# Context's Fourier part in seven steps, a transform and the gate's turns reordered, matrices by casting DMA

## The chip, the cores and the metric

The program runs on one core of a Trainium2 chip. The metric is device time in microseconds of one execution. The engines are TensorE (PE: matmuls, with weight loads as PEld), VectorE (DVE), ScalarE (ACT), GpSimd (POOL) and SyncE (SP). SP and POOL issue the DMAs here, each from a queue that goes in order. Line numbers such as L322 are those of the kernel before.

## The reference, cut to what matters

Two layers over 1024 latent tokens and 256 context tokens with 1024 channels. The first layer is projected once (`u @ w_in`); 512 channels go to a Fourier mix, three times 512 to a two-stage Hyena convolution. The second layer, neighbourhood attention, and the gated feed-forward parts lie behind what is changed.

```python
def fourier_mix(p):
    g = p.astype(jnp.float32).reshape(B_, L, FOURIER_GROUPS, FOURIER_GDIM).transpose(0, 2, 1, 3)
    f = jnp.fft.fft2(g, norm="ortho").real
    return f.transpose(0, 2, 1, 3).reshape(B_, L, FOURIER_CH).astype(p.dtype)

def hyena_mix(p, conv_w, conv_b, w1, b1, freq, w2, b2, w3, skip):
    z = short_conv(p, conv_w, conv_b).astype(jnp.float32)
    x1, x2, v = jnp.split(z, 3, axis=-1)
    filt = hyena_filters(L, w1, b1, freq, w2, b2, w3)
    v = x1 * long_conv(v, filt[:, 0], skip[0])
    v = x2 * long_conv(v, filt[:, 1], skip[1])
    return v.astype(p.dtype)

def mixer_ab(u, w_in, w_out, ...):
    p = u @ w_in
    y_f = fourier_mix(p[..., :FOURIER_CH])
    y_h = hyena_mix(p[..., FOURIER_CH:], ...)
    return jnp.concatenate([y_f, y_h], axis=-1) @ w_out
```

Both streams, latent and context, go through `mixer_ab` with the same weights. Context is the short one: 256 tokens.

## The kernel before, in words

Activations lie with channels on the 128 partitions and tokens along the rows. Matmul operands are split into a rounded high part (a copy on ScalarE, L326) and a rest (a subtraction on VectorE, L328), and each product is three matmuls: high by high, low by high, high by low.

The functions are Python generators. The order in which the builder draws from them is the order of the program, and so a priority; when the program is built, a scheduler fixes each engine's order and the buffers from it and from its own estimate of times. `follow(ins)` puts an instruction behind another one on the same engine, without a wait. On the chip every engine and queue takes its instructions strictly in the order fixed.

`in_proj` runs 16 blocks (steps 0 to 15) of 128 output channels. A step loads and splits a weight block, runs its 72 matmuls (`lin`), draws one step of the context filters (`filt`) and of the modulation vectors (`ada`), draws from `four` and `conv` from a given step on, and evicts its own result: blocks 0 to 3 for the Fourier part, the others through the short convolution (L814 to L818). Context's blocks 0 to 3 are stored to memory (`pd`).

`fourier_c` is context's Fourier part in four groups of 128 channels. For each group it loads two halves, folds them (`folded`), splits three operands, multiplies them by the channel matrix (`channels`), splits the three results, multiplies those by the position matrices, and evicts (`fourier_out`). All of a group is in one step; a last step multiplies the middle column (`middle`) and writes the results.

`conv` is context's long convolution: `forward_c` turns the operand (L899), then transforms two classes of frequencies, `cls` 0 and 1; `combine_c` multiplies by the filter's spectrum; `inverse_c` goes back. `o` is the first or second convolution. A class's matrices (`vf_c`) are loaded as float16 and cast on ScalarE: at L365 into S2 buffers for `o` 0, at L374 otherwise.

The latent long convolution begins with `turned` (L981), which transposes the operand into eight tiles and splits them. Eight `unit`s follow, each a class and a block of frequencies: a first half of the matmuls, a second half, then `combine_l` (L949 to L958), which loads the spectrum and multiplies, and `parts` (L970, L972), which splits. A unit of class 1 has 24 matmuls and two matrices, one of class 0 has 12 and one. After each unit of the first convolution a gate tile is turned (`turn_x`, L1006). `inverse_first` transforms back, applies the gate and forms the next operand; while it ends, the first four units of the second convolution are begun (first halves). `inverse_last` (L1111) ends the second convolution, with the latent Fourier part in it.

What matters of the buffers: S2 has 35 (512 words a row, whatever is asked for), S4 has 21 (1024 words), `wh` and `wl` two each, `ws` four (staging of float16 matrices and of weights); of the eight PSUM banks six are `ps` and two `pq`. Behind the projection `self.PS` gives `ps` alone, and `self.PQ` gives `pq`. `cmat` and `cmat2` load a float16 matrix into `ws` from SP and cast it on ScalarE (L374, L388) into `wh` or `wl`. `cast` has GpSimd issue a DMA that casts on its way into the buffer (L313).

Of the kernel before, what the change touches and what calls it, by code (L numbers as in the profile page):

```python
# [10 lines left out]
F32 = mybir.dt.float32  # L11
F32R = mybir.dt.float32r
# [6 lines left out]
P = 128  # L19
# [217 lines left out]
class Builder:  # L237
# [154 lines left out]
    def cast(self, w, src):  # L392

        self.mj = (self.mj + 1) % 4
        m = self.W(("wh", "ws", "wl", "ws")[self.mj], "mat", F32R, w)
        self.ldr(m, src)
        return m

# [422 lines left out]
    def in_proj(self, u, fill, four, conv):  # L821
# [14 lines left out]
        for i, nb in enumerate(order):  # L836
            wh, wl = self.weights(a["w_in"][nb])
            acc = self.lin(wh, wl, 0, range(KB), u, PCS)
            for g, n in fill:
                for _ in range(n[min(i, len(n) - 1)]):  # L840
                    next(g, None)
            if i > 5:
                next(four, None)
            if i > 13:
                next(conv, None)
# [45 lines left out]
    def forward_c(self, o):  # L891
        nc, a = self.nc, self.a
        ab = self.ab["c"]
        tr = []
        PS = self.PS if o == 0 else self.PQ
        for j in (0, 1):
            ps = PS()
            for cb in range(4):
                nc.tensor.transpose(ps[:, cb * P:(cb + 1) * P], ab[cb][:, j * P:(j + 1) * P], self.ident)  # L899
            hi, lo = self.twin(o)  # L900
            self.split(ps, hi, lo)
            tr.append((hi, lo))
        yield
        for cls in (0, 1):
            spec = []
            for i in (cls, 2 + cls):
                xh, xl = tr[(i + i // 2) % 2]
                mt = self.cmat(256, a["vf_c"][i, 0], small=o == 0)
                ps = PS()
                self.mm(ps, mt[:, :P], xh, True, False)  # L910
                self.mm(ps, mt[:, :P], xl, False, False)
                self.mm(ps, mt[:, P:], xh, False, True)
                spec.append(ps)
            self.combine_c(o, cls, spec)
            yield
# [58 lines left out]
    def turned(self):  # L974

        nc = self.nc
        self.tr = []
        for j in range(8):
            ps = self.PS()
            for cb in range(4):  # L980
                nc.tensor.transpose(ps[:, cb * P:(cb + 1) * P], self.ab["l"][cb][:, j * P:(j + 1) * P], self.ident)  # L981
            hi, lo = self.S2(F32R), self.S2(F32R)
            self.split(ps, hi, lo)
            self.tr.append((hi, lo))
            yield
# [14 lines left out]
    def turn_x(self, k):  # L1000

        pc, rev, j = k // 4, k // 2 % 2, k % 2
        ps = self.PQ()
        for cb in range(4):
            x = (self.xrev if rev else self.xrow)[cb][:, j * P:j * P + P]
            self.nc.tensor.transpose(ps[:, cb * P:(cb + 1) * P], x, self.ident)  # L1006
        t = self.S2()
        self.nc.scalar.copy(t, ps)
        self.xt[(j, (0, 1, 2, 3)[2 * pc + rev])] = t

    def unit(self, o, fb, cls, bank=None):

        a = self.a
        tr = self.tr
        if cls == 0:
            src = a["vfe_l"][fb]
            mt = self.cast(1024, src) if o + fb == 0 else self.cmat(1024, src)
            mats = [mt[:, :512], mt[:, 512:]]
            q = 2 * (fb // 2)
            xs = [range(q, q + 2), range(4 + q, 6 + q)]  # L1020
        else:
            src = a["vfo_l"][fb]
            mats = [self.cast(1024, src[:, j * 1024:j * 1024 + 1024]) for j in (0, 1)] if o + fb == 0 else self.cmat2(src)
            xs = [range(4, 8), range(4)]
        bank = bank or self.PS
        spec = [bank(), bank()]
# [335 lines left out]
    def fourier_c(self, y):  # L1362
# [4 lines left out]
        for i in range(3):  # L1367
# [1 line left out]
            self.ldr(m[:, :256], a["fc_c"][i, 0])  # L1369
            self.ldr(m[:, 256:], a["fc_c"][i, 1])  # L1370
            mats[i] = m
        raws = []
        for g in range(4):
            p0, p1 = self.S2(F32, 128), self.S2(F32, 128)
            self.ld(p0, self.pd[g][:, 0:128])
            self.ld(p1, self.pd[g][:, 128:256])
            prs = self.folded(p0, p1, P, q[:, g:g + 1], qn[:, g:g + 1], nc.gpsimd)
            ae, ao, am = self.channels(prs, cg, 1, self.PS)
            ps = self.PS()
            for i, (xh, xl) in enumerate((ae, am, ao)):  # L1380
                m = mats[i]
                self.mm(ps[:, :256], xh, m[:, :256], i == 0, False)
                self.mm(ps[:, :256], xl, m[:, :256], False, False)
                self.mm(ps[:, :256], xh, m[:, 256:], False, i == 2)
            raw = self.S2()
            self.fourier_out(ps[:, 0:128], ps[:, 128:256], raw, P, self.T)
            raws.append(raw)
            yield
        self.middle(cgf, q, qn, mid, self.PS)
        for g in range(4):  # L1390
            nc.vector.tensor_copy(raws[g][:, P:P + 1], mid[:, g:g + 1])
            self.split(raws[g][:, :256], y.ap(0, g, 2), y.ap(1, g, 2))
# [771 lines left out]
    def run(self):  # L2164
# [119 lines left out]
                pass  # L2284

        self.banks = 6
        next(cc, None)
        self.xt, self.sums_due = {}, None
        for _ in self.turned():
            pass  # L2290
        for k, (fb, cls) in enumerate(((0, 1), (0, 0), (1, 1), (1, 0), (2, 1), (3, 1), (2, 0), (3, 0))):
# [2 lines left out]
            if k % 4 == 0:  # L2294
                self.gate_rows(k // 4)
            self.turn_x(k)
            if k == 6:
                next(cc)
        self.parts()
        units = [self.unit(1, fb, cls, self.PQ if k == 3 else None)  # L2300
                 for k, (fb, cls) in enumerate(((0, 1), (1, 1), (2, 1), (0, 0), (1, 0), (3, 1), (2, 0), (3, 0)))]
        for _ in range(2):
            next(cc)
# [259 lines left out]
```

## Time and profile before

| | |
|---|---|
| median of 3 runs | 2956.7 us (2954.18 to 2958.66) |
| the profiled execution's own time | 2957.89 us |
| its span, first to last instruction | 2956.0 us |
| mean granted TensorE clock | 0.984 |

In the views, times are microseconds from the span's start. A row of the timeline gives start, length, engine, line, operation, output and inputs by the program's names, shapes and count, and in brackets how long the engine had been idle and what released it. A row of the stages gives the busy time of PE, PEld, DVE, ACT and POOL, the granted clock, the share of the DMA engines and GB/s. The instructions that the change touches lie in about 290 to 640 us.

### The profile page before, as it was taken

The numbers are of one execution on the slowest core, as the hardware profiler recorded it, in microseconds if no ns is written. First come the engines' busy times: TensorE is split into PE (matmuls) and PEld (weight loads), VectorE is DVE, ScalarE is ACT, GpSimd is POOL, SyncE is SP. The second block draws the span as 40 slices with busy tenths as digits, with TensorE's granted clock in tenths as the row PEclk, the third lists the DMA queues.
The fourth block names the chain that finished last, engine by engine and source line by source line (L and its number), as shares of the span: only waits on it lengthen the run. The fifth ranks groups of instructions, "written<-read, shape, count | busy, mean of one in ns | idle before, by whom it ended". The sixth has DMA issues, their size and how long they took to land. (4 is left out here: it accounts for less than half of the span.)

```text
span 2956.0 us, 44485 instructions
## 1 busy us (share of the span) xinstructions
PE 2832.5 (96%) x15704; PEld 2363.7 (80%) x15704; DVE 2092.7 (71%) x3950; ACT 1330.1 (45%) x2490; POOL 529.2 (18%) x820
## 2 busy tenths in 40 slices
PE   8899898899999999999999999999999999999998
PEld 3678787788799888888888888788877688888886
DVE  6765666858777888966777437888777877764555
ACT  4543323543454333333455336677665533333433
POOL 2112012351100221222120002232212022111000
PEclk9999999999999999999999999999999999999999
DMA  9664433566556555659984345676756266434653
GB/s 336 219 210 161 144 102 127 185 222 225 199 176 199 193 202 202 219 189 323 309 305 153 129 130 154 174 183 168 221 169 226 75 240 227 168 111 167 227 194 128
DMA packets 303917, 568.41 MB, mean 192 GB/s; under 512 B 83144, under 2 KB 129930, under 8 KB 303694
## 3 DMA queue, kind: packets, MB, share of 16 engines
q1 hardware_dynamic: 242750, 373.11, 39.7%
q0 software_dynamic: 58640, 188.26, 17.8%
q10 hardware_dynamic: 2304, 4.20, 0.4%
q8 instruction: 124, 2.03, 0.3%
q14 instruction: 99, 0.81, 0.1%
HBM read 415.49 MB, written 119.80 MB: 181 GB/s over the span
## 5 line engine op out<-in xcount | busy, mean ns | idle before, releaser
L1605 PE MATMUL ps<-s,s 128*128 128x512 f32 x2008 | 498.3, 391 | 6.4 <-DVE s L1496 4.7
L1605 PEld LDWEIGHTS ps<-s,s 128*128 128x128 f32 x2008 | 377.6, 188 | 88.3 <-DVE s L1496 6.3
L322 PE MATMUL ps<-s,wh 128*128 128x256 f32 (+1 forms) x1584 | 358.7, 329 | 3.5 <-ACT wh L326 3.4
L322 PE MATMUL pq<-s,wh 128*128 128x512 f32 (+1 forms) x1040 | 316.2, 381 | 9.8 <-DVE s L1990 4.7
L322 PEld LDWEIGHTS ps<-s,wh 128*128 128x128 f32 x1584 | 265.8, 192 | 29.6 <-ACT wh L326 4.7
L322 PE MATMUL ps<-s,s 128*128 128x64 f16 (+3 forms) x2780 | 243.8, 241 | 31.1 <-DVE s L2099 8.8
L1777 PE MATMUL ps<-s,s 128*128 128x512 f32 (+1 forms) x1000 | 259.6, 383 | 3.1 <-DVE s L328 3.0
L328 DVE TENSOR_TENSOR wl<-ws,wh 128x1024 fp32r<-128x1024 f32 (+1 forms) x142 | 170.0, 1198 | 127.5 <-ACT wh L326 123.0
L326 ACT CAST wh<-ws 128x1024 fp32r<-128x1024 f32 (+1 forms) x142 | 145.8, 1027 | 241.2 <-PE ps L322 91.8
L326 ACT CAST s<-s 128x1024 fp32r<-128x1024 f32 (+2 forms) x184 | 168.1, 940 | 191.3 <-DMA s<-d 162.6
L322 PE MATMUL ps<-s,wl 128*128 128x256 f32 (+1 forms) x792 | 238.4, 327 | 2.7 <-DVE wl L328 2.7
L322 PEld LDWEIGHTS pq<-s,wh 128*128 128x128 f32 x1040 | 190.8, 191 | 47.5 <-DVE s L1990 5.9
L326 ACT CAST s<-t 128x512 fp32r<-128x512 f32 (+1 forms) x213 | 121.9, 587 | 220.9 <-PE ps L1605 81.2
L328 DVE TENSOR_TENSOR s<-s,s 128x1024 fp32r<-128x1024 f32 (+2 forms) x162 | 185.5, 1177 | 49.4 <-ACT s L326 46.9
L1777 PEld LDWEIGHTS ps<-s,s 128*128 128x128 f32 x1000 | 184.5, 188 | 41.2 <-DVE s L328 4.6
L322 PE MATMUL ps<-s,mat 128*128 128x512 f32 x714 | 180.3, 402 | 18.1 <-ACT s L326 10.9
L322 PE MATMUL pq<-s,wl 128*128 128x512 f32 (+1 forms) x520 | 196.3, 379 | 1.3 <-DVE wl L328 1.3
L328 DVE TENSOR_TENSOR s<-t,s 128x512 fp32r<-128x512 f32 (+1 forms) x213 | 136.9, 653 | 78.9 <-ACT s L326 51.0
L1605 PE MATMUL ps<-s,wh 128*128 128x512 f32 x608 | 189.1, 390 | 0.0
L322 PEld LDWEIGHTS ps<-s,mat 128*128 128x128 f32 x714 | 135.6, 193 | 54.9 <-ACT s L326 13.5
L322 PEld LDWEIGHTS ps<-s,s 128*128 128x128 f32 (+1 forms) x860 | 133.9, 196 | 45.3 <-ACT s L326 10.9
L322 PEld LDWEIGHTS ps<-s,wl 128*128 128x128 f32 x792 | 148.8, 191 | 16.4 <-DVE wl L328 3.6
(439 smaller groups left out, 5614.9 us busy)
## 6 DMA issues: line engine op xcount, KB each, us to landing
s<-d SPq DMA_DIRECT2D x283, 256.0 KB, 3.8
s<-in_down SPq DMA_DIRECT2D x150, 256.0 KB, 4.1
d<-s POOLq DMA_DIRECT2D x137, 256.0 KB, 3.3
s<-in_ada_w POOLq DMA_DIRECT2D x64, 512.0 KB, 5.2
d<-tk POOLq DMA_DIRECT2D x98, 256.0 KB, 3.6
g<-in_bias SPq DMA_DIRECT2D x128, 192.0 KB, 3.1
ws<-in_up SPq DMA_DIRECT2D x44, 512.0 KB, 3.9
d<-g POOLq DMA_DIRECT2D x87, 256.0 KB, 3.1
```

What stands on the lines that cost most here:

```text
L322: self.nc.tensor.matmul(o, l, r, start=st, stop=sp)
L326: self.last_hi = nc.scalar.copy(hi, src).ins
L328: self.last_lo = eng.tensor_tensor(lo, src, hi.bitcast(F32), SUB).ins
L1605: nc.tensor.matmul(ps, x[:, sl], y, start=first and j == 0 and x is wh and y is xh, stop=j == 3 and x is wl, skip_group_check=True)
L1777: m = nc.tensor.matmul(acc[j][:, c0:c1], x[:, sl], y[:, xs], start=first and k == 0, stop=last and k == 2, skip_group_check=True)
```

## The change

- Context's Fourier part begins one step earlier (step 5 instead of 6) and goes in seven steps: step k folds group k, multiplies group k-1 by the channel matrix and group k-2 by the position matrices, and evicts group k-3. The middle and the final splits are two further steps.
- `forward_c`'s class 1 of the first convolution is drawn after unit 1 instead of ahead of `turned`.
- The gate's turns are put behind the last transpose of `turned` on TensorE.
- `vf_c`'s matrices of the first convolution come by a casting DMA from GpSimd into S2. So do those of units 2 and 3 of the second convolution, into S4 (`cast4`), where SP and ScalarE brought them into `wh` and `wl`.
- Unit 7 of the second convolution, like unit 3, takes its banks from `pq`.

```diff
+    def cast4(self, src):
+
+        m = self.S4(F32R)
         self.ldr(m, src)
         return m
...
-            if i > 5:
+            if i > 4:
                 next(four, None)
             if i > 13:
                 next(conv, None)
...
-                mt = self.cmat(256, a["vf_c"][i, 0], small=o == 0)
+                if o == 0:
+                    mt = self.S2(F32R, 256)
+                    self.ldr(mt, a["vf_c"][i, 0])
+                else:
+                    mt = self.cmat(256, a["vf_c"][i, 0])
...
-                nc.tensor.transpose(ps[:, cb * P:(cb + 1) * P], self.ab["l"][cb][:, j * P:(j + 1) * P], self.ident)
+                last = nc.tensor.transpose(ps[:, cb * P:(cb + 1) * P], self.ab["l"][cb][:, j * P:(j + 1) * P], self.ident)
+            self.after_turned = last.ins
...
-            self.nc.tensor.transpose(ps[:, cb * P:(cb + 1) * P], x, self.ident)
+            with self.follow(self.after_turned):
+                self.nc.tensor.transpose(ps[:, cb * P:(cb + 1) * P], x, self.ident)
...
-    def unit(self, o, fb, cls, bank=None):
+    def unit(self, o, fb, cls, bank=None, wide=False):
...
-            mt = self.cast(1024, src) if o + fb == 0 else self.cmat(1024, src)
+            mt = self.cast4(src) if wide else self.cast(1024, src) if o + fb == 0 else self.cmat(1024, src)
...
-            mats = [self.cast(1024, src[:, j * 1024:j * 1024 + 1024]) for j in (0, 1)] if o + fb == 0 else self.cmat2(src)
+            half = [src[:, j * 1024:j * 1024 + 1024] for j in (0, 1)]
+            mats = [self.cast4(x) for x in half] if wide else [self.cast(1024, x) for x in half] if o + fb == 0 else self.cmat2(src)
...
-        raws = []
-        for g in range(4):
-            p0, p1 = self.S2(F32, 128), self.S2(F32, 128)
-            self.ld(p0, self.pd[g][:, 0:128])
-            self.ld(p1, self.pd[g][:, 128:256])
-            prs = self.folded(p0, p1, P, q[:, g:g + 1], qn[:, g:g + 1], nc.gpsimd)
-            ae, ao, am = self.channels(prs, cg, 1, self.PS)
-            ps = self.PS()
-            for i, (xh, xl) in enumerate((ae, am, ao)):
-                m = mats[i]
-                self.mm(ps[:, :256], xh, m[:, :256], i == 0, False)
-                self.mm(ps[:, :256], xl, m[:, :256], False, False)
-                self.mm(ps[:, :256], xh, m[:, 256:], False, i == 2)
-            raw = self.S2()
-            self.fourier_out(ps[:, 0:128], ps[:, 128:256], raw, P, self.T)
-            raws.append(raw)
+        raws, prs, opd, got = [], {}, {}, {}
+        for k in range(7):
+            if k >= 3:
+                raw = self.S2(F32, 256)
+                ps = got.pop(k - 3)
+                self.fourier_out(ps[:, 0:128], ps[:, 128:256], raw, P, self.T)
+                raws.append(raw)
+            if 0 <= k - 2 < 4:
+                ae, ao, am = opd.pop(k - 2)
+                ps = got[k - 2] = self.PS()
+                for i, (xh, xl) in enumerate((ae, am, ao)):
+                    m = mats[i]
+                    self.mm(ps[:, :256], xh, m[:, :256], i == 0, False)
+                    self.mm(ps[:, :256], xl, m[:, :256], False, False)
+                    self.mm(ps[:, :256], xh, m[:, 256:], False, i == 2)
+            if 0 <= k - 1 < 4:
+                opd[k - 1] = self.channels(prs.pop(k - 1), cg, 1, self.PS)
+            if k < 4:
+                p0, p1 = self.S2(F32, 128), self.S2(F32, 128)
+                self.ld(p0, self.pd[k][:, 0:128])
+                self.ld(p1, self.pd[k][:, 128:256])
+                prs[k] = self.folded(p0, p1, P, q[:, k:k + 1], qn[:, k:k + 1], nc.gpsimd)
             yield
         self.middle(cgf, q, qn, mid, self.PS)
+        yield
...
         self.banks = 6
-        next(cc, None)
         self.xt, self.sums_due = {}, None
...
-            if k == 6:
+            if k in (1, 6):
                 next(cc)
         self.parts()
-        units = [self.unit(1, fb, cls, self.PQ if k == 3 else None)
+        units = [self.unit(1, fb, cls, self.PQ if k % 4 == 3 else None, k in (2, 3))
```

More of the change, by code (lines that the diff above doesn't have):

```diff
@@ L395, in cast @@
         m = self.W(("wh", "ws", "wl", "ws")[self.mj], "mat", F32R, w)
+        self.ldr(m, src)
+        return m
+    def cast4(self, src):
+        m = self.S4(F32R)
         self.ldr(m, src)
```

## The prediction

> **What bounds the kernel now.** I read the page's head first, then busy time and granted clock by stage, then, in each stage that the change touches, TensorE's waits, its clock in stretches of one clock step, and the instructions around each wait in order of time.
>
> ```profile
> span 2956.0 us, 44485 instructions
> ...
> PE 2832.5 (96%) x15704; PEld 2363.7 (80%) x15704; DVE 2092.7 (71%) x3950; ACT 1330.1 (45%) x2490; POOL 529.2 (18%) x820
> ```
>
> TensorE is busy for 96% of the span, so a microsecond counts only if TensorE gets it. By stage (columns: stretch, its length, busy time of each engine with instruction counts, granted TensorE clock, DMA share, GB/s):
>
> ```profile
> 320.00:400.00 80.00, 70.51 (x369) 59.69 (x369) 46.02 (x153) 23.74 (x56) 4.74 (x5) 0.94 0.38 126
> ...
> 474.00:493.00 19.00, 10.99 (x56) 9.08 (x55) 14.42 (x24) 9.57 (x17) 5.03 (x4) 0.82 0.29 97
> 493.00:560.00 67.00, 64.81 (x316) 53.79 (x317) 48.15 (x62) 36.33 (x51) 32.27 (x28) 1.00 0.57 181
> 560.00:620.00 60.00, 48.65 (x205) 38.89 (x204) 42.36 (x55) 26.86 (x32) 18.11 (x12) 0.94 0.57 193
> 620.00:700.00 80.00, 79.05 (x535) 72.42 (x534) 57.31 (x107) 35.04 (x61) 31.72 (x41) 1.00 0.70 242
> ```
>
> TensorE idles 9.5 us in 320:400 (in-projection with context's Fourier groups in it), 8.0 us in 474:493 (change-over to the latent convolution) and 11.4 us in 560:620 (from the first convolution's inverse to the second's units), and next to nothing in 620:700. In the same three stages the clock is below 1. So each stall may cost twice, once as idle time and once as work at half clock:
>
> ```profile
> 327.60:331.00 3.40, 3.36 (x15) 3.37 (x16) 1.28 (x5) 0.88 (x4) 0.00 (x0) 0.51 0.02 5
> 368.60:372.00 3.40, 3.40 (x19) 3.40 (x18) 0.92 (x4) 0.80 (x3) 0.00 (x0) 0.50 0.00 0
> 392.50:395.90 3.40, 3.40 (x17) 3.37 (x17) 0.46 (x2) 0.13 (x1) 0.00 (x0) 0.50 0.04 15
> 481.20:488.00 6.80, 5.52 (x20) 4.87 (x21) 6.26 (x13) 1.90 (x4) 0.88 (x1) 0.50 0.51 174
> 580.20:583.60 3.40, 2.93 (x8) 2.25 (x8) 3.40 (x6) 1.74 (x3) 0.00 (x0) 0.50 1.06 402
> 614.40:617.80 3.40, 3.40 (x9) 2.65 (x8) 3.40 (x4) 0.00 (x0) 2.85 (x2) 0.50 0.10 37
> ```
>
> TensorE is nearly always busy in these, at 0.50: half of that busy time is lost.
>
> **Part A, Fourier part as a pipeline.** TensorE's waits in 320:400 (total us, times, longest), and two stalls:
>
> ```profile
> PE ps L322 <- ACT s L326: 5.2, 6, 1.6
> ...
> PE pq L322 <- DVE wl L328: 1.3, 1, 1.3
> ```
> ```profile
> 326.49 0.91 PE L322 MATMUL ps<-s,s 128*128 128x256 f32 x3 [1.63 <-ACT s L326]
> ...
> 390.28 0.58 PE L322 MATMUL ps<-s,s 128*128 128x256 f32 x2 [1.21 <-ACT s L326]
> ```
>
> Within one step the old code loads, folds, splits, multiplies, splits again and multiplies again, and TensorE stands in front of each split (`ps<-s,s`, 256 wide, is `channels`). In the new code every product uses what an earlier step split, and between two steps lie the 72 matmuls of a projection block. No matmul is added. Gone are the 5.2 us of waits and half of 3.36, 3.40 and 3.40, 5.1 us: at most 10.3. A wait like the second row's stays, and it is of the size of those that go (1.3 against 1.21 and 1.63), so I leave one of the three slow stretches, 1.7 us: **8.6 us** (2.6 if new waits replace half of them and the clock falls as before; 10.3 if all goes). Loads, folds and evictions that now start a step earlier (also six matrix loads on GpSimd's queue) lie under the projection: VectorE is busy 46.0 of 80 us here, GpSimd 4.7. If that cover is gone, the second rival below holds.
>
> **Part B, the turns.** TensorE from the projection's end to the first convolution unit, with the casts it waits for:
>
> ```profile
> 475.79 0.60 PE L1006 MATMUL pq<-c,g 128*128 128x128 f32 x4
> 482.48 1.09 PE L1006 MATMUL pq<-c,g 128*128 128x128 f32 x4 [6.09 <-DVE s L816]
> 483.21 2.91 PE L322 MATMUL ps<-s,s 128*128 128x512 f32 x6
> 485.92 3.83 PE L981 MATMUL ps<-c,s 128*128 128x128 f32 x24
> ...
> 492.92 1.28 PE L322 MATMUL ps<-s,mat 128*128 128x512 f32 x3
> ```
> ```profile
> 485.00 0.21 DVE L817 SCALAR_TENSOR_TENSOR s<-ps,c,s 128x1 f32<-128x1 f32 x1
> ...
> 489.68 0.62 ACT L326 CAST s<-t 128x512 fp32r<-128x512 f32 x1 [0.64 <-POOL t L935]
> 490.21 4.00 ACT L326 CAST s<-ps 128x512 fp32r<-128x512 f32 x8
> 490.94 4.87 DVE L328 TENSOR_TENSOR s<-ps,s 128x512 fp32r<-128x512 f32 x8
> ```
>
> A gate's turn (L1006) waits 6.09 us for a bank that the last short convolution (L816, L817) still holds; the latent transposes (L981) stand behind it; their eight casts then stand behind the cast of context's second class (489.68), which waited for GpSimd. The change takes the turn and that class (the six matmuls at 483.21) out from before them. The transposes can go at 476.4. Not all of the 9.5 us from there to 485.92 come free: VectorE is in the short convolution until 485.2, so the low parts (4.87 us) start there and not at 490.94: 5.7 us earlier. The six matmuls and eight turns come back inside the units, where TensorE is the bound: 6 x 0.23 (pace of the row at 598.76 below) and 2 x 0.60 = 2.6. Net **3.1 us**. Ends: -2.6, if ScalarE's order keeps the casts where they are; +8.6, if the casts slip in ahead of the short convolution, 5.5 us earlier still. The new order on TensorE holds up only what is queued behind the turns, the units' matmuls; the turned gate is wanted first by the inverse, at the end of the units' 67 us. The moved class brings VectorE some 4 us (six passes of 0.6 to 0.7, as for the 4.87 us of eight), two loads on SyncE's queue and two on GpSimd's into 493:560, where VectorE has 18.9 us free.
>
> **Part C, the second convolution's units.** TensorE, then who it waits for:
>
> ```profile
> 579.57 0.73 PE L322 MATMUL ps<-s,mat 128*128 128x512 f32 x2 [3.88 <-ACT s L326]
> 580.77 6.63 PE L322 MATMUL ps<-s,mat 128*128 128x512 f32 x22 [0.47 <-ACT s L326]
> 589.11 5.28 PE L322 MATMUL ps<-s,mat 128*128 128x512 f32 x22 [1.71 <-ACT mat L388]
> ...
> 598.76 9.68 PE L322 MATMUL ps<-s,mat 128*128 128x512 f32 x42
> ...
> 613.89 4.58 PE L322 MATMUL ps<-s,mat 128*128 128x512 f32 x12 [4.57 <-DVE s L949]
> ...
> 619.54 0.72 PE L1111 MATMUL ps<-mat,s 128*128 128x256 f32 x4 [0.71 <-ACT s L970]
> ```
> ```profile
> 602.05 6.31 SPq L307 DMA_DIRECT2D s<-d  x8
> ...
> 604.77 1.23 DVE L949 TENSOR_TENSOR s<-pq,s 128x1024 f32<-128x1024 f32 x1 [3.49 <-DMA s<-d]
> ...
> 612.52 1.22 DVE L949 TENSOR_TENSOR s<-ps,s 128x1024 f32<-128x1024 f32 x1 [3.47 <-DMA s<-d]
> ```
>
> Four units are begun ahead, but their seven cast matrices share four slots (two tags, two buffers each). So TensorE runs dry while the inverse's last tiles are split (3.88 + 0.47) and again for a cast (1.71). With units 2 and 3 in S4 buffers their first halves, 12 + 6 matmuls at 0.23, 4.1 us, fill the first stall, and the second has no cause: 6.1 plus half of 2.93, 7.6. The last unit on the PQ banks can run its 12 matmuls in the 4.57 us gap: 4.57 plus half of 3.40, 6.3. Together 13.9. What is next late is VectorE's product with the filter's spectrum (L949): it waited 3.49 and 3.47 us for loads that SyncE issues behind eight others, and its parts end the 0.71 us wait at 619.54. I let these three stand on the path: 13.9 - 7.7 = **6.2 us** (0 if the loads keep their places in time; 13.9 if they move up with TensorE, whose progress frees the buffers that they fill).
>
> **The casting loads.**
>
> ```profile
> mat<-in_vfo_l POOLq DMA_DIRECT2D x2, 512.0 KB, 3.4
> cs<-in_vfo_l SPq DMA_DIRECT2D x7, 512.0 KB, 4.0
> ```
> ```profile
> L388 ACT CAST mat<-cs x33: 1039/1049/1055, 459.1 to 660.0; 128x1024 fp32r<-128x1024 f16 x33
> L365 ACT CAST s<-s x4: 405/410/427, 462.8 to 482.7; 128x256 fp32r<-128x256 f16 x4
> ```
>
> Three large and four small matrices lose their cast, some 4.8 us of ScalarE, which is 45% busy, and gain a GpSimd issue each. I cost them at nothing; the exposure, if one lands late, is its 3.4 us. The Trainium skill, "DMA: Bandwidth & Descriptors", section "Specifications", speaks against the move: 1 us to the first byte on GpSimd's path, 0.6 on SyncE's. By that figure seven loads would take 2.8 us more. The trace doesn't agree: the same matrix landed in 3.4 us from GpSimd, cast, and in 4.0 from SyncE.
>
> **Sum.** 8.6 + 3.1 + 6.2 = 17.9 us off the profiled execution's own 2957.9 (span 2956.0 and 1.9 around it; 1.2 above the median of the runs, inside their spread of 4.5): **2940.0 us**. Behind 620 TensorE is 99% busy, so what is gained arrives at the end.
>
> **Rivals.**
>
> *The loads keep their time.* SyncE's queue issues in order, and the spectrum loads come when the queue comes to them. Then part C gives nothing and B and A remain: 2957.9 - 11.7 = 2946. For it: both waits at L949. Against it: the queue itself waits for buffers that TensorE frees. 0.20.
>
> *S2 buffers run short, and it gets slower.* Between steps the pipeline holds 12 S2 tiles more (three operand pairs in each of two stages) of 35. By the code the context filters, still running in steps 5 to 9, with the context's inputs (8), tables, modulation rows and the short convolution's three tiles can hold some 30. If the short convolution's tiles wait, it keeps its banks and TensorE stops: at the price of one old stall, 1.63 and half of 3.36, 3.3 us a step. Five steps cost 16.5 and part A gains nothing: 2957.9 - 9.3 + 16.5 = 2965. It decides from the third such step on (9.3 / 3.3). Against it: a tile's load and fold are no longer urgent and can wait. 0.17.
>
> *The clock doesn't follow these stalls.* If the half-clock stretches have another cause than the waits, they stay, and A loses 3.4 and C, where 1.5 and 1.7 were counted, 3.2: 2946.6. The Trainium skill, "TensorE: Matmul & The Clock Gate", section "Part 1: The HAM clock gate", says that the clock halves after an idle window of about 3.4 us. By that rule stalls of 1.2 to 1.6 us would not do it; the trace disagrees, as a slow stretch follows at 327.60 and at 392.50, within 2.3 us of their ends (326.49 and 390.28). 0.08.
>
> *The order doesn't change where it matters.* Each engine's order is planned when the kernel is built; if the plan puts other waits in the same places, nothing moves: 2957. 0.10.
>
> **How the numbers follow.** The forecast has 0.45, its own range 2930 (A and C at their upper ends, 9.4 more) to 2952 (A and B at their lower ends, 11.7 less). With the rivals the range is 2927 (B and C at their upper ends, 13.2 more) to 2966; it leaves out the far half of the slow case and greater gains. A measurement of this kernel tells about 0.2% (5.9 us) from no change. Faster: 0.45 + 0.20 + 0.08, less 0.01 for small gains, 0.72; same 0.10 and that 0.01; slower 0.17.
>
> **What would show it.** A: no `ps<-s,s` wait over 1 us between 300 and 400, and a clock of 0.98 or more there; wrong, if waits on VectorE's short convolution or on S2 loads stand there instead. B: L981 right behind the projection, first unit at 486 to 488 on the old scale, L1006 without a wait. C: no wait for `mat` or L949 between the units; wrong, if the inverse's L1111 starts as late after the units as before. The forecast falls if the three stages together lose less than 7 us, or the stages behind 700 differ by more than 5.

## The result, and the profile after

The changed kernel takes 2953.3 us (median of 20 runs, 2945.8 to 2967.5; before 2957.2). The ratio is 0.9988, 95% interval 0.9977 to 1.0000. 17.9 us were forecast; 3.9 came.

The head of the page of after, then its stages on its own time axis (columns as for before):

```profile
span 2965.7 us, 44508 instructions
...
PE 2840.9 (96%) x15704; PEld 2372.0 (80%) x15704; DVE 2091.5 (71%) x3950; ACT 1324.0 (45%) x2483; POOL 532.1 (18%) x827
```
```profile
320.00:400.00 80.00, 77.96 (x433) 67.64 (x432) 58.20 (x176) 25.46 (x56) 6.61 (x8) 1.00 0.48 158
460.00:477.00 17.00, 10.07 (x54) 8.77 (x52) 12.91 (x22) 10.66 (x20) 2.49 (x2) 0.70 0.21 70
477.00:546.00 69.00, 63.57 (x300) 52.73 (x299) 46.33 (x55) 33.65 (x44) 38.10 (x35) 0.95 0.62 195
546.00:610.00 64.00, 54.31 (x229) 43.08 (x228) 48.31 (x64) 25.88 (x30) 18.49 (x12) 0.94 0.59 201
610.00:690.00 80.00, 77.63 (x514) 70.59 (x514) 54.41 (x104) 34.53 (x59) 29.13 (x41) 0.98 0.67 225
690.00:720.00 30.00, 26.16 (x135) 21.88 (x135) 24.68 (x66) 10.15 (x17) 3.27 (x6) 0.94 0.53 204
```

The first stage is nearly full (78.0 of 80 us) at full clock. The change-over is as idle as before (6.9 of 17 us) and slower (0.70). The first units, which were at 1.00, stand at 0.95; the second units stay at 0.94; and behind them TensorE has 26.2 of 30 us in 690:720, at 0.94, where before had 27.7 in 700:730, at 1.00.

This execution is the slowest of the 20, and a span can't say where time went. For that I take the start of the n-th recorded matmul (every trace has 15704) in both traces. The lead of a kernel is how much earlier that matmul starts than before's, less the same difference at before's 290 us, ahead of everything changed (-2.3 to +4.4 us in these traces). Columns are before's times; "end" is the last matmul but three. Beside these medians before took 2956.5 to 2958.3 on the same chips. A number that falls from left to right is time given back. Two traces in which TensorE has one order up to 754 (`four_only` and `four_rot`) differ by up to 1.8 in these columns, so a difference of that size says nothing. Where an expectation below does not say "counted from 290 us", its leads are without the subtraction.

| kernel | 471 | 512 | 592 | 634 | 674 | 754 | end | median, us |
|---|---|---|---|---|---|---|---|---|
| changed, first trace | 16.0 | 10.2 | 19.4 | 11.9 | 12.2 | 6.3 | -7.3 | 2953.3 |
| changed, second (`after_again`) | 16.2 | 11.3 | 20.6 | 12.9 | 13.7 | 5.5 | 3.5 | 2953.4 |
| `four_only` | 15.9 | 15.8 | 16.3 | 16.6 | 16.1 | 15.8 | 16.7 | 2943.0 |
| `class_back` | 16.1 | 14.1 | 22.0 | 11.8 | 10.1 | 7.0 | 6.6 | 2952.4 |
| `class_cmat` | 16.3 | 12.8 | 22.3 | 14.5 | 15.7 | 11.0 | 8.3 | 2940.7 |
| `back_cmat` | 16.0 | 15.5 | 23.3 | 13.2 | 14.1 | 11.0 | 8.1 | 2948.8 |
| `no_wide` | 15.7 | 10.8 | 11.8 | 10.0 | 10.8 | 12.1 | 11.5 | 2947.9 |
| `no_pq7` | 16.0 | 10.6 | 20.3 | 15.1 | 13.8 | 8.6 | 7.4 | 2953.7 |
| `nowide_tk` | 16.0 | 17.7 | 17.1 | 15.5 | 16.3 | 17.7 | 15.4 | 2940.6 |
| `four_wide` | 16.1 | 14.6 | 22.7 | 17.3 | 16.6 | 12.3 | 16.5 | 2945.1 |
| `wide_spec` | 16.0 | 14.6 | 22.8 | 14.0 | 14.0 | 10.8 | 18.5 | 2946.3 |
| `four_rot` | 16.0 | 14.8 | 14.9 | 14.8 | 14.3 | 15.6 | 15.4 | 2941.7 |
| `wide_nofill` | 16.4 | 15.1 | 23.4 | 17.5 | 16.1 | 17.2 | 23.4 | 2936.1 |
| `wide_keep` | 16.2 | 14.8 | 23.0 | 17.7 | 17.3 | 19.8 | 18.6 | 2938.4 |
| `after_keep` | 16.1 | 11.3 | 20.7 | 13.0 | 13.9 | 12.1 | 8.1 | 2950.4 |
| `after_fixed` | 15.9 | 18.2 | 24.4 | 13.7 | 13.3 | 14.7 | 10.6 | 2949.2 |
| `fixed_no_pq7` | 16.1 | 17.6 | 24.1 | 18.4 | 18.1 | 20.5 | 21.1 | 2941.0 |

So the change gains 16 us in the projection and gives it back in three places: some 5 at the change-over (471 to 512), 7.5 of the 9 it gains up to 592 again by 634, and 6 to 8 in the output projection (674 to 754).

Line numbers in a run's views are those of its own kernel: L991, L1018, L959 and L1124 of after are the L981, L1006, L949 and L1111 of before, and the products of L959 are L955 in `four_wide` and `wide_spec`.

**The change-over.** TensorE in after, the load on GpSimd's queue, and two stretches by engine and clock:

```profile
463.69 1.25 PE L991 MATMUL ps<-c,s 128*128 128x128 f32 x8 [0.51 <-DVE t L943]
471.36 3.67 PE L991 MATMUL ps<-c,s 128*128 128x128 f32 x16 [6.42 <-DVE s L328]
474.83 1.87 PE L1018 MATMUL pq<-c,g 128*128 128x128 f32 x8
476.39 8.49 PE L322 MATMUL ps<-s,mat 128*128 128x512 f32 x36
484.73 0.84 PE L322 MATMUL ps<-s,s 128*128 128x512 f32 x3
...
490.90 1.65 PE L322 MATMUL ps<-s,s 128*128 128x512 f32 x3 [4.45 <-DMA s<-in_vf_c]
```
```profile
485.64 0.53 POOL L313 DMA_DIRECT2D s<-in_vf_c  x1 [6.22 <-PE ps L322]
```
```profile
466.30:476.50 10.20, 5.14 (x25) 5.01 (x25) 9.23 (x17) 7.72 (x17) 0.00 (x0) 0.50 0.18 65
490.20:497.00 6.80, 6.10 (x14) 4.84 (x15) 4.72 (x7) 0.62 (x1) 6.01 (x4) 0.50 0.17 64
```

The latent transposes (L991) do go first, but after 16 of them they wait 6.42 us for a low part that frees a bank; the stall has changed its owner, no more. The first unit starts only 3 us earlier for that. Then the moved class waits 4.45 us for a matrix that GpSimd issues at 485.64, right behind TensorE's three matmuls of 484.73; it had waited 6.22 us for TensorE to be done with a buffer. TensorE is at half clock from 490.2 to 497.0.

**The second units.** TensorE, then VectorE's products with the spectrum (L959):

```profile
581.23 8.46 PE L322 MATMUL ps<-s,mat 128*128 128x512 f32 x36 [0.81 <-ACT mat L374]
...
592.18 4.61 PE L322 MATMUL ps<-s,mat 128*128 128x512 f32 x12 [2.49 <-DVE s L959]
598.10 3.00 PE L322 MATMUL pq<-s,mat 128*128 128x512 f32 x12 [1.31 <-DVE s L959]
603.33 0.74 PE L1124 MATMUL ps<-mat,s 128*128 128x256 f32 x4 [2.23 <-DVE s L966]
...
608.04 10.29 PE L1124 MATMUL ps<-mat,s 128*128 128x256 f32 x66 [1.69 <-ACT s L980]
```
```profile
590.90 1.23 DVE L959 TENSOR_TENSOR s<-ps,s 128x1024 f32<-128x1024 f32 x1 [2.71 <-DMA s<-d]
596.74 1.22 DVE L959 TENSOR_TENSOR s<-pq,s 128x1024 f32<-128x1024 f32 x1 [2.34 <-DMA s<-d]
```

The wait for `mat` is down from 1.71 to 0.81 us, and TensorE now waits for banks that the products hold, and at the inverse for what comes out of them. From 590 to 608 us its waits come to 8.9 us, where before had 5.5 ahead of and in the inverse (4.57, 0.71 and one of 0.23).

**The output projection.** TensorE's longest wait there, before and then after, each with VectorE's fullest 20 us, and the half-clock stretch around the second:

```profile
720.73 0.50 PE L1438 MATMUL ps<-s,wh 128*128 128x256 f32 x2 [2.14 <-DVE s L1413]
```
```profile
720.00:740.00 20.00, 19.10 (x110) 16.61 (x111) 20.00 (x58) 7.13 (x11) 3.77 (x7) 1.00 0.42 144
```
```profile
715.90 1.01 PE L322 MATMUL ps<-s,wl 128*128 128x256 f32 x2 [3.69 <-DVE wl L328]
```
```profile
700.00:720.00 20.00, 16.16 (x79) 13.23 (x79) 20.00 (x58) 4.79 (x9) 3.27 (x6) 0.91 0.32 112
715.50:718.90 3.40, 3.00 (x10) 2.62 (x11) 3.40 (x10) 0.70 (x2) 1.08 (x2) 0.50 0.53 177
```

VectorE is busy for all of one 20 us stretch in both. In after TensorE waits there for the low part of a weight, 3.69 us, and is at half clock around the end of that wait.

### The profile page after: what moved, and what is told of

Read it like the earlier page. It is cut to its first block, busy times and chain, and to the rows that moved or that the text cites. A ratio compares the mean times of both kernels' runs of the same rounds, so it can differ in the third digit from the quotient of the medians.

```text
span 2965.7 us, 44508 instructions
## 1 busy us (share of the span) xinstructions
PE 2840.9 (96%) x15704; PEld 2372.0 (80%) x15704; DVE 2091.5 (71%) x3950; ACT 1324.0 (45%) x2483; POOL 532.1 (18%) x827
## 3 DMA queue, kind: packets, MB, share of 16 engines
q0 software_dynamic: 59648, 190.36, 18.1%
## 5 line engine op out<-in xcount | busy, mean ns | idle before, releaser
L1625 PE MATMUL ps<-s,s 128*128 128x512 f32 x1956 | 485.4, 390 | 2.8 <-DVE s L1516 2.3
L1625 PEld LDWEIGHTS ps<-s,s 128*128 128x128 f32 x1956 | 367.8, 188 | 80.4 <-DVE s L1516 3.0
L322 PE MATMUL ps<-s,wh 128*128 128x256 f32 (+1 forms) x1700 | 385.0, 331 | 5.0 <-ACT wh L326 3.6
L322 PEld LDWEIGHTS ps<-s,wh 128*128 128x128 f32 x1700 | 283.9, 191 | 36.6 <-ACT wh L326 5.5
L322 PE MATMUL pq<-s,wh 128*128 128x512 f32 (+1 forms) x924 | 282.6, 383 | 6.9 <-DVE s L2010 4.6
L322 PE MATMUL ps<-s,s 128*128 128x64 f16 (+3 forms) x2777 | 244.5, 241 | 35.3 <-DVE s L2119 10.2
L322 PE MATMUL ps<-s,wl 128*128 128x256 f32 (+1 forms) x850 | 254.1, 331 | 6.2 <-DVE wl L328 6.2
L1797 PEld LDWEIGHTS ps<-s,s 128*128 128x128 f32 x1000 | 184.6, 188 | 40.9 <-DVE s L328 4.4
L322 PEld LDWEIGHTS pq<-s,wh 128*128 128x128 f32 x924 | 171.3, 193 | 39.3 <-DVE s L2010 5.9
L322 PE MATMUL ps<-s,mat 128*128 128x512 f32 x678 | 174.2, 405 | 11.6 <-ACT s L326 7.2
L322 PEld LDWEIGHTS ps<-s,wl 128*128 128x128 f32 x850 | 158.7, 192 | 22.3 <-DVE wl L328 6.9
L322 PE MATMUL pq<-s,wl 128*128 128x512 f32 (+1 forms) x462 | 174.5, 380 | 0.0
```

What stands on the lines that cost most here:

```text
L322: self.nc.tensor.matmul(o, l, r, start=st, stop=sp)
L1625: nc.tensor.matmul(ps, x[:, sl], y, start=first and j == 0 and x is wh and y is xh, stop=j == 3 and x is wl, skip_group_check=True)
L1797: m = nc.tensor.matmul(acc[j][:, c0:c1], x[:, sl], y[:, xs], start=first and k == 0, stop=last and k == 2, skip_group_check=True)
```

## The experiments

**The change again, and its parts alone or undone.** `after_again` is the changed kernel.

> The changed kernel once more, to see which differences between the two traces repeat. Theory (the pipeline gains some 16 us by the end of the projection; the moved class gives 6 back; out_proj, bound by VectorE, gives 6 more back): against the kernel before, the first MATMUL of the turns (L991) comes 13 to 17 us earlier, the second pair of class-1 products again waits over 3 us for a matrix from GpSimd's queue, and the first in_proj-of-FFN matmuls behind out_proj come 2 to 6 us earlier. Rival (the give-back in out_proj was chance): the 10 us that it starts early are still there behind it. Time 2951 to 2956.

2953.4 us (0.9976 to 1.0002). Each of the three losses is there again, so none is the chance of one execution. The "end" column is less firm: the two traces of this one program differ by 11 there.

`four_only`: the kernel before with the new `fourier_c` and

```diff
-            if i > 5:
+            if i > 4:
                 next(four, None)
```

> The kernel before with nothing but context's Fourier pipeline. Theory: the projection's end comes 14 to 17 us earlier, the turns' stall of 6.1 us stays, and some 10 of these microseconds arrive before out_proj, of which it gives back up to 6: 2945 to 2952. Rival 1 (out_proj sets a time of its own and takes all): 2955 to 2958. Rival 2 (nothing is lost behind the projection): 2941 to 2943.

2943.0 us, ratio 0.9956 (0.9942 to 0.9969). Its lead stays at 16 to the end. Rival 2 holds: nothing is lost behind the projection. So the output projection does not take a gain back as such, and the rest of the change costs some 10 us.

`class_back`: in the changed kernel the class's `next(cc)` stands ahead of `turned` again (`if k == 6` below).

> The changed kernel with context's second class drawn ahead of the turns again, as before; its matrices still come by casting DMA, and the rest of the change stays. Theory (moved behind the second unit, the class meets full S2 buffers): the wait of 4.45 us for in_vf_c goes, at 512 us the kernel is 13 to 16 us ahead of the kernel before and not 8, and the time falls by 2 to 6 us against the changed kernel, to 2947 to 2951. Rival (the casting loads are slow wherever they stand): a wait for in_vf_c of over 2 us stays, now ahead of the turns, and the time is that of the changed kernel, 2953.

`class_cmat`: the changed kernel with

```diff
-                if o == 0:
-                    mt = self.S2(F32R, 256)
-                    self.ldr(mt, a["vf_c"][i, 0])
-                else:
-                    mt = self.cmat(256, a["vf_c"][i, 0])
+                mt = self.cmat(256, a["vf_c"][i, 0], small=o == 0)
```

> The changed kernel with the four small matrices of context's transform loaded as 16-bit numbers by SyncE and cast by ScalarE, as before. Theory (full S2 buffers): each now needs two buffers and not one, the wait of 4 us or more behind the second unit stays or grows, 2953 to 2957. Rival (GpSimd's issue and its casting path cost the 4.45 us): the wait goes, 2947 to 2950.

`back_cmat`: both of these together.

> The changed kernel with the whole of part B's class move and the small casting loads undone: context's second class ahead of the turns, its four matrices through SyncE and ScalarE; the Fourier pipeline, the order of the gate's turns behind the latent ones, the wide units and the last unit's PQ banks stay. Theory (the moved class loses 4 to 6 us to full S2 buffers, and each of the two edits alone takes only a part of that back): 17 to 20 us ahead of the kernel before at 512 us, no wait over 1 us for a class matrix; time 2938 to 2944. Rival (the loss sits in the units and the output projection, whatever the classes do): 15 to 17 ahead at 512 but 8 or less at 754; 2948 to 2953.

Between 471 and 512 the changed kernel loses 5 to 6 us, `class_back` 2.0, `class_cmat` 3.5, `back_cmat` 0.5; kernels with before's order there lose 0.1 to 1.5. So both edits together take the loss back; `class_back` alone comes close to that, `class_cmat` takes back a part. In `class_back` nothing waits for a class matrix any more. `class_back`'s time hardly moved (2952.4; 0.9967 to 0.9991), against the theory, since later stages gave the lead back. `class_cmat` took 2940.7 (0.9933 to 0.9967, four runs), against the theory too, though its matrices still make TensorE wait 2.50 us; its trace is the slowest of the four, and its time is 6 us better than its lead of 11 at 754 explains. With four runs I leave that open.

**Where the moved class's wait comes from.** `nowide_tk` is `no_wide` (below) with one word changed:

```diff
-                    mt = self.S2(F32R, 256)
+                    mt = self.TK(F32R, 256)
```

> The changed kernel without the wide units (2947.9 us; between 471 and 512 us it loses 4.8 us against the kernel before), with the four small matrices of context's transform in the TK buffers instead of S2; they still come from GpSimd, cast on the way, behind the second unit. Theory (a full S2 pool delayed the load): the wait of some 4 us for the last matrix is gone, and between 471 and 512 it loses 1 us or gains up to 2; 2940 to 2944. Rival (casting loads from GpSimd are slow there): the wait stays over 2.5 us, 2946 to 2949.

2940.6 us (0.9935 to 0.9971, four runs). TK is another pool, of four buffers. The loads are the same, from GpSimd. The last of them as it is issued; TensorE; and the loads in 440:500:

```profile
460.95 0.53 POOL L313 DMA_DIRECT2D tk<-in_vf_c  x1 [7.40 <-PE ps L322]
```
```profile
483.94 1.53 PE L322 MATMUL ps<-s,tk 128*128 128x512 f32 x6
```
```profile
tk<-in_vf_c POOLq DMA_DIRECT2D x4, 128.0 KB, 3.3
```

TensorE does not wait. The loads took 3.3 us from issue to landing as a median, and 3.2 in after, so they are no faster. What differs is the issue: the last load goes out at 460.95, 23 us ahead of its use, and not at 485.64, when its use was due. The S2 buffer that was still held was the cause. With it out of the way part B gains 1.7 us (16.0 to 17.7) where it lost 4.9; in `after_fixed` and `fixed_no_pq7` below, also with TK buffers, it gains 2.3 and 1.5.

**The units.** `no_wide`: the changed kernel without `k in (2, 3)`. `no_pq7`: the changed kernel with `self.PQ if k == 3`. `four_wide`: `four_only` with `cast4` and `k in (2, 3)`.

> The changed kernel with the matrices of units 2 and 3 through ScalarE's cast again. Against the changed kernel's second profile (20.4 us ahead of the kernel before at 592 us, 12.7 at 634, 5.4 at 754). Theory (fixed chain): 12 to 14 ahead at 592, still 12 to 14 at 634, time as the changed kernel's, 2951 to 2955. Rival 1 (wide buffers harm the loads): 15 or more ahead at 634, time 2946 to 2949. Rival 2 (wide is worth its 8 us): 5 or less ahead at 634, 2959 to 2961.

> The changed kernel with the last unit on PS banks again. Against the changed kernel's second profile (17.0 us ahead of the kernel before at 614 us, 12.7 at 634). Theory (fixed chain): 12 to 14 ahead at 634, a stall before the last unit in place of stalls behind it, 2951 to 2955. Rival (the last unit on the PQ banks holds them from the inverse and the stages behind): 15 or more ahead at 634, stall-free output projection, 2944 to 2949.

> The kernel before with context's Fourier pipeline and the wide matrices of units 2 and 3, nothing else. Against the pipeline alone (2943.0 us; 17.9 us ahead of the kernel before at 592 us, 18.2 at 634, 17.4 at 734). Theory (a fixed chain, spectrum loads and VectorE's products, sets the end of the second units, so what TensorE gains ahead of them is waited away): 6 to 8 us more at 592, at most 1.5 more at 634; time 2941 to 2945. Rival 1 (the three S4 buffers make the spectrum loads later): less than 17 ahead at 634, time 2946 to 2952. Rival 2 (the wide units' gain lasts): 24 ahead at 634, 2935 to 2938.

`no_wide` took 2947.9 (0.9957 to 0.9982), 5.5 less than the changed kernel, `no_pq7` 2953.7 (0.9971 to 0.9997), `four_wide` 2945.1 (0.9940 to 0.9973). `no_pq7` has the theory's time, but is 2 to 3 us further ahead at 634, between theory and rival. The wide units gain 8 us by 592 and lose 5.4 of it by 634 in `four_wide`, so the theory's chain holds in the main; the remaining 2.7 are lost in the output projection, with 1.6 more. `no_wide` has the theory's lead at 592 and nearly at 634 (13.0 and 11.2 without the subtraction), but not its time: it lost nothing between 674 and 754 and ended ahead. That pointed to the output projection.

`wide_spec`: `four_wide` with the second convolution's spectrum on another queue.

```diff
-        self.ld(two(F), d[0:2].rearrange("e p c -> p e c"))
+        (self.ldr if o else self.ld)(two(F), d[0:2].rearrange("e p c -> p e c"))
```

> The Fourier pipeline and the wide units alone (2945.1 us; counted from 290 us, 22.8 us ahead of the kernel before at 592 us, 17.3 at 634, 12.4 at 754), with the second convolution's spectrum loads issued by GpSimd instead of SyncE. Theory (the third and fourth spectrum loads had a free buffer for 30 us and stood on SyncE behind four matrix loads that wait for ScalarE's casts): the products (L955) no longer wait for DMA there, where they waited 3.0 and 1.9 us, and the lead at 634 is 20 to 23. Rival 1 (the chain of products, sums and parts is full without those waits): 16 to 18 at 634. Rival 2 (GpSimd's own queue holds them up as long): waits of 2 us or more at L955 stay. Time 2939 to 2943 by the theory, 2944 to 2947 by the rivals.

2946.3 us. The products of `four_wide`, then of `wide_spec`:

```profile
581.12 1.22 DVE L955 TENSOR_TENSOR s<-ps,s 128x1024 f32<-128x1024 f32 x1 [2.97 <-DMA s<-d]
586.50 1.23 DVE L955 TENSOR_TENSOR s<-pq,s 128x1024 f32<-128x1024 f32 x1 [1.90 <-DMA s<-d]
```
```profile
585.00 1.23 DVE L955 TENSOR_TENSOR s<-ps,s 128x1024 f32<-128x1024 f32 x1 [1.75 <-DMA s<-d]
589.53 1.23 DVE L955 TENSOR_TENSOR s<-pq,s 128x1024 f32<-128x1024 f32 x1 [1.04 <-DMA s<-d]
```

The two waits shrink from 4.9 to 2.8 us together, and the lead at 634 is 3 us smaller, not larger. The theory falls: over 40% of the loads' lateness went and nothing came of it. Rival 1 had 16 to 18 at 634 and Rival 2 waits of 2 us or more, so neither of them came either. Which link sets the chain is not settled.

**The output projection.** `four_rot`: `four_only` and, ahead of `inverse_first`,

```diff
+        for _ in range(3):
+            self.nc.gpsimd.memset(self.S4()[:, :1], 0.0)
```

> The Fourier pipeline alone (2943.0 us; counted from 290 us, 16.1 us ahead at 674 us and 15.8 at 754), with three S4 buffers drawn and left empty where the wide matrices would draw theirs. Kernels with wide units lose 3 to 8 us in the output projection (674 to 754), kernels without none. Theory (three buffers further round the ring, the loads of the modulation rows find other buffers and the order there changes for the worse): 3 to 6 us lost between 674 and 754, TensorE's wait there is for a low part (wl) and over 2.5 us; 2946 to 2950. Rival (it is what TensorE gains ahead of it that the stage takes back): nothing lost, 2942 to 2945.

`wide_nofill` is `four_wide` without part of the work, so its time is no candidate:

> The Fourier pipeline and the wide units alone, with VectorE's products of the fifth modulation group left out of the output projection (its columns are set to zero, its weights are still loaded). Theory (VectorE, full from 700 to 720, sets TensorE's wait of 2.9 us there): no TensorE wait over 1 us between 674 and 754, the lead of 16.6 us at 674 (counted from 290) is still 16 or more at 754; 2939 to 2942. Rival (the loads at 99% of the DMA engines set it): the wait stays, now for a load or a cast behind one; 2944 to 2947.

`four_rot` took 2941.7 (0.9936 to 0.9967) and lost nothing: the S4 ring is not it. `wide_nofill` took 2936.1 (0.9915 to 0.9961), its lead rises from 16.1 to 17.2 across the stage, and no TensorE wait over 0.5 us is left in it: VectorE's 32 products are what the low part waits for. Among all other kernels, VectorE has one of two orders between 674 and 754: before's, or another in which a weight's low part stands behind more products. The other one is found wherever the wide units draw fewer weight buffers. The eight traces with it lose 3.1 to 8.2 us in this stage, the eight others with before's order between -2.5 and 1.8. `wide_keep` (on `four_wide`) and `after_keep` (on the changed kernel) draw those again and leave them empty:

```diff
         if cls == 0:
             src = a["vfe_l"][fb]
+            if wide:
+                self.W("ws", "cs", F16, 1024)
+                self.mat(1024)
...
             src = a["vfo_l"][fb]
+            if wide:
+                self.W("ws", "cs", F16, 2048)
+                self.mat(1024)
+                self.mat(1024)
```

> The Fourier pipeline and the wide units alone (2945.1 us; counted from 290 us, 16.6 us ahead of the kernel before at 674 us, 12.3 at 754), and the wide units draw the weight buffers (two ws, three of wh and wl) that their cast matrices took, and leave them empty. Theory (the turned ring of weight buffers gives VectorE the worse order in the output projection): with the ring as it was, TensorE's wait for wl of 2.9 us goes, the lead at 754 is 16 to 17.5; 2939 to 2943. Rival (the wide units' earlier arrival makes the loss): the lead falls by 3 us or more between 674 and 754 again, 2944 to 2947.

> The changed kernel, its wide units drawing the weight buffers that their cast matrices took, and leaving them empty. Changed kernel: counted from 290 us, 12.2 and 13.7 ahead at 674 us in two profiles, 6.3 and 5.5 at 754; 2953.3 us. Theory: no loss in the output projection, 11.5 to 14 ahead at 754, 2944 to 2948. Rival (the loss has another cause): 5 to 8 ahead at 754, 2951 to 2955.

Both have before's order. In `four_wide` ScalarE begins the weight's high part at 694.50, VectorE its low part 6 us later, and TensorE waits:

```profile
694.50 1.05 ACT L326 CAST wh<-ws 128x1024 fp32r<-128x1024 f32 x1 [1.22 <-PE ps L1452]
...
700.53 1.22 DVE L328 TENSOR_TENSOR wl<-ws,wh 128x1024 fp32r<-128x1024 f32 x1
...
701.80 1.01 PE L322 MATMUL ps<-s,wl 128*128 128x256 f32 x2 [2.86 <-DVE wl L328]
```

and in `wide_keep`:

```profile
698.88 1.05 ACT L326 CAST wh<-ws 128x1024 fp32r<-128x1024 f32 x1 [3.10 <-PE ps L1459]
...
703.52 1.23 DVE L328 TENSOR_TENSOR wl<-ws,wh 128x1024 fp32r<-128x1024 f32 x1
...
704.81 0.62 PE L322 MATMUL ps<-s,wl 128*128 128x256 f32 x2 [0.18 <-DVE wl L328]
```

`wide_keep` gains 2.5 us across the stage where `four_wide` lost 4.3, and takes 2938.4 (0.9921 to 0.9948, four runs), 14.9 us below the changed kernel. It is the lowest median here of a kernel that does all the work, but its interval overlaps those of `four_only` and `four_rot`, and by a little `four_wide`'s; the cause is shown by the stage in the traces, not by the medians. `after_keep` loses 1.8 where the changed kernel lost 6 to 8; at 2950.4 (0.9957 to 0.9984) it came out above the theory's 2944 to 2948, its lead falling from 12.1 to 8.1 behind 754.

**Both repairs, and the PQ banks.** `after_fixed` is the changed kernel with TK buffers and kept weight buffers; `fixed_no_pq7` puts its last unit back on PS banks.

> The changed kernel with both repairs: context's class matrices in TK buffers, and the weight buffers drawn as before. Theory (the losses are separate and add up): counted from 290 us, 17 to 18 ahead at 512 us, 24 to 26 at 592, 17 to 19 at 634, 16 to 19 at 754; time 2938 to 2942, as the changed kernel without wide units and with TK buffers (2940.6 us), since the wide units' gain is still waited away. Rival (the repairs overlap, or the wide units' loss grows by what the others free): 13 or less at 754, 2944 to 2948.

> The changed kernel with both repairs (class matrices in TK buffers, weight buffers drawn as before) and the last unit on PS banks again. Theory (the last unit on the PQ banks costs 2 us or more at 634 us: with it the kernels lost 7.5 to 10.7 us between 592 and 634, without it 5.2 to 5.5): counted from 290 us, 24 to 25 ahead at 592, 18.5 to 20 at 634, 18 to 22 at 754; time 2936 to 2941, with the pipeline and the kept weight buffers alone (2938.4 us) or better. Rival (the PQ banks do not matter; the turned order or the class move feeds the loss): 15 or less ahead at 634, as with both repairs alone (13.7), 2946 to 2950.

`after_fixed`, 2949.2 (0.9965 to 0.9990), was too high by the theory: it has its 18.2 at 512 and 24.4 at 592, and keeps 13.7 of them at 634. `fixed_no_pq7` keeps 18.4, as the theory said, and takes 2941.0 (0.9928 to 0.9969). With the last unit on PQ banks the stretch from 592 to 634 gives back 7.5 to 10.7 us where the wide units are in, without it 5.2 to 5.9 (all but `wide_spec`); so that edit costs 2 to 5 us there. In time, `fixed_no_pq7` is 8 us below `after_fixed`, but `no_pq7` is no better than the changed kernel.

## Why the prediction was wrong, by its own steps

**Part A: right in kind, too small.** Forecast 8.6 with an upper end of 10.3; it is 16 in every trace (15.7 to 16.4). The term mis-sized is the stall: I took one row, ScalarE's splits (5.2 us), and counted none of the others of that view as a gain. They are waits for banks that the context filters' evictions hold (L794, L797) and for a weight's two parts. Before, in 300:440, there were also:

```profile
PE pq L322 <- ACT s L794: 2.1, 3, 0.7
PE pq L322 <- DVE wl L328: 1.3, 1, 1.3
PE pq L322 <- ACT wh L326: 0.7, 1, 0.7
PE pq L322 <- DVE s L797: 0.7, 1, 0.7
```

After, these two rows are all that is left:

```profile
PE ps L322 <- DVE s L328: 1.4, 1, 1.4
PE pq L322 <- ACT s L800: 0.7, 1, 0.7
```

So a group that bunches its splits on ScalarE and VectorE seems also to delay what its neighbours need of them; `four_only` shows that the pipeline alone removes these waits, not by which link. TensorE's idle time in that stretch fell by 8.2 us (busy 129.72 to 137.96 of 140) and all three half-clock stretches went, 5.1 more. The rest, some 2.6, is busy time without a cause shown: the same 714 matmuls from 290 us on took 139.8 us of busy time before and 132.1 after, 7.7 less, of which the clock explains 5.1. The signs named for it came: no `ps<-s,s` wait over 1 us, clock 1.00.

**Part B: the step that failed is "the casting loads, at nothing".** The order came as forecast, L991 right behind the projection and the turns without a wait, and the first unit started 3 us earlier (forecast 5.7, at 490 on the old scale, not 486 to 488, as the transposes' banks wait for low parts). But the exposure that I put at 3.4 us "if one lands late" was a wait of 4.0 to 4.7 in all five traces that have the class there with casting loads in S2, with half clock behind it. I had seen S2's shortage as a rival and put it in steps 5 to 9, where nothing of it showed; it stood one stage later, where I had cleared the moved class by VectorE's free time and its queues and not by its buffers. The gain of 3.1 became a loss of 5.

The two rows by which I put the loads' path at nothing were also misread: they are not the same matrix. A row's KB counts the buffer that is written, so 512 KB from GpSimd are one half of the matrix, 1024 numbers a row as 32-bit, and 512 KB from SyncE the whole, 2048 as 16-bit. Loads of one size are `vfe_l`'s in before: 2.5 us from SyncE (`cs`, 256 KB, median of seven), 3.4 from GpSimd (`mat`, 512 KB, one load), 0.9 longer. The small matrices took 2.6 us from SyncE before and 3.2 from GpSimd after. The trace did show the slower path, then; but with the same path and no held buffer `nowide_tk` has no wait, so this was not what cost the 4 to 5 us.

**Part C: the rival "the loads keep their time" was right in its result, not in its cause.** The 7.6 us of the wide units are there at 592 (8 measured); the second units give back most of it by 634, where `four_wide` is only 0.7 ahead of `four_only`. The step that failed is to count the filled gap of 4.57 us as a gain: the waits moved on, to the banks and to the inverse, and the two products still wait 2.71 and 2.34 us for their loads (3.49 and 3.47 before). I had taken 7.7 off for three waits and let the rest stand as gain; yet in `wide_spec`, with two of them cut by over 40%, nothing came, so the loads alone do not set that chain. The last unit on PQ banks, priced at a gain of 6.3, costs 2 to 5 up to 634.

**The sum: "what is gained arrives at the end" failed.** It was read from 620:700 alone. The stage behind it has VectorE full for 20 us, and it lost 6 to 8 us. The rule holds for a kernel that comes into the stage with the same order: `four_only` keeps its 16 us, `wide_keep` its 17. It does not when the edit also changes the order far away: five weight buffers fewer (two `ws`, three of `wh` and `wl`), and VectorE puts a low part behind products that nobody waits for. My rivals had an order that stays as it was, not one that changes elsewhere. In the two traces: 16 in the projection, 5 to 6 lost at the change-over, 2 gained with all the units, 6 to 8 lost in the output projection, which leaves 6.3 and 5.5; the medians say 4. That the total is a gain at all is luck as far as the forecast goes: with the 8.6 of part A in place of 16 these figures would leave a loss of 1 to 2 us.

**Open.** From 754 us to the end the changed kernel loses 13.6 and 2.0 us more in its two traces. One suspect is again the last unit's PQ banks: between 1600 and 2000 us TensorE has before's order in all eight kernels without that edit, and another one in all nine traces with it. The nine lose 0.4 to 13.6 us more from 754 to the end, the eight between 1.2 and, as a gain, 7.7. That order may cost some us; but the two traces of one program lie 11.6 apart there and `no_pq7`'s median is not lower, so it is not shown.

## What to carry to other kernels

Price a moved step by the buffers that its loads need at the new place, not only by the engines and queues it passes: a load whose buffer is still held is late by that, however fast its path. An edit that draws fewer tiles from a shared ring can reorder a stage that it never touches, so read the order on the fullest engine there, and keep the ring turning if the new order is worse. And time each part alone: the pipeline by itself was worth nearly four times the whole change (14.4 us against 3.9).

## What the runs showed of the hardware that was not expected

Half-clock stretches come in steps of 3.4 us and need no idle stretch of that length: before, waits of 1.63 and 1.21 us (until 326.49 and 390.28) were each followed by one, while a wait of 2.14 us in before's output projection (L1438, until 720.73) was followed by none. Two executions of the one changed program had a mean clock of 0.979 and 0.984, which over their spans is 62 against 47 us of clock not granted; their times differ by 13. The Trainium skill, "TensorE: Matmul & The Clock Gate", section "Part 1: The HAM clock gate", says that the activity window runs freely and does not start with the kernel; the differing executions agree with that. The same page of the Trainium skill, section "Part 4: PE-mode transpose", says that a transpose doesn't count as busy in the same way; the longest half-clock stretch of the change-over, 10.2 us from 466.3, holds the transposes, but also the stall of 6.42 us, so it can't tell the two apart.
